# A two-layer decoder trunk: the feed-forward's operands turned by VectorE and DRAM instead of TensorE

## The chip, the cores and the metric

The kernel runs on one core of a Trainium2 chip. The metric is the device time of one execution in microseconds (us), the median of several runs.

## What is computed

The reference is a decoder trunk of depth 2 over 256 tokens with 2048 channels in float32. Layer 0 mixes tokens by stick-breaking attention, layer 1 by a gated DeltaNet; behind each mixer stands a dense SwiGLU feed-forward with 5632 hidden columns. Cut to what matters here:

```python
def swiglu(h, w_gu, w_down):
    gate, up = jnp.split(h @ w_gu, 2, axis=-1)
    return (jax.nn.silu(gate) * up) @ w_down
...
    for i in range(DEPTH):
        kind, j = i % N_MIXERS, i // N_MIXERS
        h = rms_norm(x, mix_norm[i])
...
        x = x + y.astype(x.dtype)
        x = x + swiglu(rms_norm(x, ffn_norm[i]), ffn_w_gu[i], ffn_w_down[i]).astype(x.dtype)
```

## The kernel before

**Products.** Each large product is a list of blocks of 512 output columns for all 256 tokens, and each block a list of units, two 128-row steps of the weights each. A float32 operand is split into a high part in the reduced type fp32r and a low part, the rest; a product is then three: high by high, high by low, low by high. A unit's weights (128 x 1024, 512 KB) come by one DMA on SP's queue (`load`), ScalarE writes their high part, VectorE subtracts to get the low part (`convert`), and TensorE makes 12 matmuls of 512 columns (`product`). The other operand, activations with the channel on the partition, lies in SBUF, split in advance: hTh and hTl for the normed input, and pairs kh and kl for the hidden values.

**The feed-forward.** The 5632 hidden columns are 11 blocks of 512 (j = 0 to 10). For j = 1, 3, 5, 7, 9 gate and up are plain blocks (`ffn_plain`). For the six even j they are made by a seven-product scheme (`ffn_seven`): `sums` forms sums of quarters of the weights on VectorE, and TensorE makes 21 matmuls of 256 columns a unit. Three lanes hold the weights: "a" (tiles w0 to w3) before and after, "s" (the same memory) for the seven-product units, and "b" for the plain units between them, with two raw buffers and two converted ones in the memory of the slabs (tiles slab and slabs). `merge` interleaves s and b units, and OTHERS lists the order of the plain work: a number j is gate and up of block j, a tuple is the part of the down product that uses those blocks.

**Turning the hidden values.** Gate and up leave values with tokens on the partition; the down product needs the hidden column there. At the end of up(j), VectorE has multiplied silu(gate) by up into two tiles of 128 tokens x 512 columns. `transposed_pairs` (L836) then, twice, takes a PSUM bank, has TensorE make four 128x128 transposes against the identity (`tr`, L345), and `split` (L363) reads the bank: ScalarE writes kh, VectorE kl. That is 8 transposes for each j. After the product with up, a seven-product block gives one of its two 128 x 1024 buffers ("duos") back before the transposes, the other behind them.

**What sets the order.** The program is written out in full by a scheduler in Python. Its clock (`self.t`) adds up a cost for each instruction (`spend`); side work runs as tasks that `yield`, and a task goes on when the clock of TensorE has passed what it waits for (`tick`, `Task.pause`). The costs therefore decide where in each engine's queue an instruction stands; they change no instruction. Each engine, and SP, then runs its queue in order and waits on semaphores. Matmuls in fp32r were costed at n / 2400 + 0.006 us for n columns, at least 0.107, and transposes at 0.107.

Of the kernel before, what the change touches and what calls it, by code (L numbers as in the profile page):

```python
# [8 lines left out]
F32 = mybir.dt.float32  # L9
# [22 lines left out]
class Slots:  # L32
# [28 lines left out]
    def put(self, *items):  # L61
        self.free.extend(items)
# [83 lines left out]
class Trunk:  # L146
# [2 lines left out]
    WIDE = 6  # L149
    PAIRS = 6  # L150
    SEVEN = (0, 2, 4, 6, 8, 10)
    OTHERS = (1, 3, (1, 3), 5, (0, 2), (5, 4), 7, (6, 7), 9, (8, 10), (9,))
    LEAD = 10
    SPARE = 4
    BEFORE = 3
# [16 lines left out]
    def __init__(self, ctx, tc, ins, out):  # L172
        self.tc, self.nc, self.ins, self.out = tc, tc.nc, ins, out
        self.tasks = []
        self.cur = None
        self.table = None
        self.t = {"pe": 0.0, "act": 0.0, "dve": 0.0, "sp": 0.0, "dma": self.FIRST}
        self.flags = set()
        self.smalls = {}
        self.persist = ctx.enter_context(tc.tile_pool(name="persist", bufs=1))  # L180
        self.ppool = ctx.enter_context(tc.tile_pool(name="psum", bufs=1, space=PSUM))
        t = self.sb
        self.xs = [t(f"x{n}", [P, NT, NB]) for n in range(4)]
        self.x = [[self.xs[n][:, i, :] for n in range(4)] for i in range(NT)]
        self.hT = []
        for k in range(KT // 2):
            hi, lo = t(f"hTh{k}", [P, 2, S], F32R), t(f"hTl{k}", [P, 2, S], F32R)
            self.hT += [(hi[:, j, :], lo[:, j, :]) for j in range(2)]
        self.pairs = Slots([(t(f"kh{k}", [P, 2, S], F32R), t(f"kl{k}", [P, 2, S], F32R)) for k in range(self.PAIRS)])
        self.slab = self.cut(t("slab", [P, 13 * NB]), NB) + self.cut(self.again("slabs", 8 * NB), NB)  # L190
        self.slabs = Slots(self.slab)
        self.allgm = [[t(f"gm{k}{hl}", [P, NB], F32R) for hl in range(2)] for k in range(1)]
        self.gms = Slots(self.allgm)
        self.lts, self.wide = Slots([]), Slots([])
        self.gdn_memory()
        self.acc = [[self.ppool.tile([P, NB], F32, name=f"acc{b}{i}") for i in range(NT)] for b in range(2)]
        self.banks = Slots([self.ppool.tile([P, NB], F32, name=f"bank{k}") for k in range(4)])
        dram = ctx.enter_context(tc.tile_pool(name="scratch", bufs=1, space=bass.MemoryType.DRAM))
        self.scratch = [dram.tile(s, F32, name=f"scratch{k}") for k, s in enumerate(([32, 1024], [8, P * (P + 1)]))]
        self.n = 0  # L200
        self.weights_memory()

# [134 lines left out]
    def mm(self, out, lhsT, rhs, start=True, stop=True, after=0.0):  # L337
        self.nc.tensor.matmul(out, lhsT, rhs, start=start, stop=stop, skip_group_check=True)  # L338
        n = rhs.free_size()
        if lhsT.dtype == F32R:  # L340
            self.spend("pe", max(0.107, n / 2400 + 0.006), after)
        else:
            self.spend("pe", max(lhsT.free_size(), n) / 600 + 0.005, after)

    def tr(self, out, in_):  # L345
        p = in_.shape[0]
        self.nc.tensor.transpose(out, in_, self.ident[:p, :p])  # L347
        self.spend("pe", 0.107)

    def dma(self, out, in_):  # L350
        self.nc.sync.dma_start(out, in_)
# [468 lines left out]

    def pair_operands(self, ops, src, gain=None, pair=None):

        hi, lo = pair or (yield from self.pairs.get())
        self.split(hi, lo, src, gain)
        left = [2]
        for j, o in enumerate(ops):
            o.hi, o.lo = hi[:, j, :], lo[:, j, :]
            o.ready = True

            def rel():  # L830
                left[0] -= 1
                if left[0] == 0:
                    self.pairs.put((hi, lo))
            o.release = rel

    def transposed_pairs(self, tok, ops, gain=None, put=None):  # L836

        for half in range(2):
# [12 lines left out]
                yield  # L851
            self.banks.put(bank)


    def ffn_units(self, layer, norm, nxt, last, before):

# [6 lines left out]
        def src(c0):  # L863
            return lambda k0, nk: [(gu[:, k0:k0 + nk, c0:c0 + NB], NB)]
# [2 lines left out]
            forms.append(Block(src(j * NB), norm.forms, gate, kind="seven", norm=norm))  # L867
            forms.append(Block(src(HID + j * NB), norm.forms, up, kind="seven", norm=norm))
        for n, what in enumerate(self.OTHERS):
            if isinstance(what, int):  # L870
                gate, up = self.ffn_plain(norm, kops[what])
                others.append(Block(src(what * NB), norm.ops, gate, norm=norm))
                others.append(Block(src(HID + what * NB), norm.ops, up, norm=norm))
                continue
            end = n == len(self.OTHERS) - 1
            rows = [4 * j + k for j in what for k in range(0, 4, 2)]
# [119 lines left out]
    def ffn_plain(self, norm, ops):  # L996
# [9 lines left out]
        def up(acc, free):  # L1006
            for t in range(NT):
                s = hold[t]
                self.stt(s, acc[t], norm.rstd[:, t:t + 1], s, ALU.mult, ALU.mult)
            free()  # L1010
            yield
            yield from self.transposed_pairs(hold, ops, put=lambda: self.slabs.put(*hold))
        return gate, up

    def ffn_seven(self, norm, ops):
# [10 lines left out]
        def up(acc, free):  # L1026
# [3 lines left out]
            for t in range(NT):  # L1030
                g, a = hold[0][:, t * NB:(t + 1) * NB], duo[:, t * NB:(t + 1) * NB]
                self.stt(g, a, norm.rstd[:, t:t + 1], g, ALU.mult, ALU.mult)
                toks.append(g)
            self.duos.put(duo)
            yield
            yield from self.transposed_pairs(toks, ops, put=lambda: self.duos.put(hold[0]))
        return gate, up

    def quarters(self, acc, free):
# [650 lines left out]
```

## Time and profile before

| | |
|---|---|
| median of 3 runs | 2718.93 us (2718.88 to 2719.63) |
| profiled execution | 2723.5 us, span 2721.8 us |
| TensorE busy | 2701.6 us, 99% |
| VectorE busy | 2140.8 us, 79% |
| ScalarE busy | 1488.1 us, 55% |
| DMA queue of SP | 494.10 MB, 60.2% of 16 engines' span |
| granted TensorE clock | 0.999 |

The page names engines PE (TensorE matmul), PEld (its weight loads), DVE (VectorE), ACT (ScalarE), POOL and SP. Matmul records overlap, because matmuls are pipelined: a record's length is not what the matmul costs, and the distance from one start to the next is. Most instructions are recorded at the line of a helper (L338 is every matmul, L347 every transpose, L316 every VectorE subtraction or sum of two tensors, L312 every ScalarE instruction, L503 every weight load), so groups are told apart by the names of their tiles: acc<-slabs,kh is a matmul into an accumulator from a converted b-lane weight and a hidden operand. The first feed-forward lies at about 440 to 1060 us, the DeltaNet stage up to about 2030, and the second feed-forward to the end.

### The profile page before, as it was taken

To read this page: it belongs to the slowest core of one execution; us is meant where nothing else is said; L and a number is where in the kernel's file an instruction comes from. 1 tells how busy PE (TensorE), PEld (TensorE's weight loads), DVE (VectorE), ACT (ScalarE), POOL (GpSimd) and SP (SyncE) were. 2 spreads that over 40 slices of the span, in tenths; PEclk is the share of its full clock that TensorE was granted. 3 is DMA by queue.
4 is the path that set the end of the run, shared out by engine and by line. 5 is a ranking of instruction groups with operands and counts; after the bars stand their busy time and mean duration, and the time that the engine had idled before them with its cause. 6 is when DMAs were issued, how large, how long until landed. Compare 5 with 4: busy or idle time off the path is not lost.

```text
span 2721.8 us, 39670 instructions
## 1 busy us (share of the span) xinstructions
PE 2701.6 (99%) x15018; PEld 2305.6 (85%) x15018; DVE 2140.8 (79%) x3379; ACT 1488.1 (55%) x1969; POOL 11.2 (0%) x95
## 2 busy tenths in 40 slices
PE   9999999999999999999999999999999999999999
PEld 7888888888888888888888888888888888888887
DVE  5555577889889896678878787987678899898975
ACT  5555566455545554555666556655565455455543
POOL 0000000000000000000000000000000000000000
PEclk9999999999999999999999999999999999999999
DMA  6555555656666666656656556556556566666664
GB/s 227 168 162 165 180 184 165 199 185 202 185 194 195 192 201 195 183 167 181 181 149 186 169 149 174 167 162 184 156 181 193 184 194 201 192 187 208 186 204 160
DMA packets 299834, 496.65 MB, mean 182 GB/s; under 512 B 37175, under 2 KB 79482, under 8 KB 299642
## 3 DMA queue, kind: packets, MB, share of 16 engines
q1 hardware_dynamic: 299594, 494.10, 60.2%
q8 instruction: 117, 1.92, 0.3%
q14 instruction: 75, 0.61, 0.1%
q10 hardware_dynamic: 48, 0.02, 0.0%
HBM read 489.33 MB, written 4.72 MB: 182 GB/s over the span
## 4 chain that ended last, share of the span: by engine, by line
PE 88%; DVE 6%; ACT 2%; DMA 2%; issue 2%; ACTq 0%; DVEq 0%
PE acc L338 72%; PE bank L338 13%; DVE w L316 4%; PE bank L347 2%; ACT w L312 1%; DVE slabs L316 1%; DMA slab<-in_ffn_w_down_dram 1%; DVE slab L316 1%; DVE x L316 0%; DMA slab<-in_ffn_w_gu_dram 0%; ACT slabs L312 0%; DVE slab L322 0%; ACT slab L312 0%; DMA x<-in_x_dram 0%; ACT hTh L312 0%
## 5 line engine op out<-in xcount | busy, mean ns | idle before, releaser
L316 DVE TENSOR_TENSOR w<-w,w 128x1024 fp32r<-128x1024 f32 (+2 forms) x750 | 950.0, 1286 | 278.9 <-ACT w L312 276.3
L312 ACT ACTIVATE w<-w 128x1024 fp32r<-128x1024 f32 (+2 forms) x654 | 805.1, 1242 | 379.5 <-PE acc L338 336.5
L338 PE MATMUL acc<-w,hTh 128*128 128x512 f32 (+1 forms) x3296 | 946.3, 371 | 2.8 <-DVE w L316 2.1
L338 PEld LDWEIGHTS acc<-w,hTh 128*128 128x128 f32 x3296 | 594.1, 189 | 108.1 <-DVE w L316 4.8
L338 PE MATMUL acc<-w,hTl 128*128 128x512 f32 (+1 forms) x1648 | 603.5, 366 | 0.0
L312 ACT ACTIVATE slabs<-slab 128x1024 fp32r<-128x1024 f32 x260 | 273.9, 1055 | 400.5 <-PE acc L338 252.4
L316 DVE TENSOR_TENSOR slabs<-slab,slabs 128x1024 fp32r<-128x1024 f32 x260 | 316.7, 1219 | 104.3 <-ACT slabs L312 103.6
L338 PE MATMUL acc<-w,kh 128*128 128x512 f32 x1152 | 361.3, 395 | 0.0
L338 PEld LDWEIGHTS acc<-w,hTl 128*128 128x128 f32 x1648 | 311.4, 189 | 50.9
L338 PE MATMUL acc<-slabs,hTh 128*128 128x512 f32 x1056 | 329.4, 393 | 3.0 <-DVE slab L316 1.7
L338 PE MATMUL acc<-slabs,kh 128*128 128x512 f32 x1024 | 321.7, 393 | 4.8 <-DVE slabs L316 3.3
L316 DVE TENSOR_TENSOR w<-w 128x256 f32<-128x256 f32 (+1 forms) x576 | 289.9, 507 | 6.6 <-DMA w<-in_ffn_w_gu_dram 1.5
L338 PEld LDWEIGHTS acc<-w,kh 128*128 128x128 f32 x1152 | 211.7, 188 | 41.5
L338 PEld LDWEIGHTS acc<-slabs,hTh 128*128 128x128 f32 x1056 | 192.8, 188 | 42.7 <-DVE slab L316 2.1
L338 PEld LDWEIGHTS acc<-slabs,kh 128*128 128x128 f32 x1024 | 187.5, 188 | 46.3 <-DVE slabs L316 8.7
L338 PE MATMUL acc<-w,kl 128*128 128x512 f32 x576 | 224.7, 390 | 0.0
L338 PE MATMUL acc<-slabs,hTl 128*128 128x512 f32 x528 | 205.7, 390 | 0.0
L338 PE MATMUL acc<-slabs,kl 128*128 128x512 f32 x512 | 199.5, 390 | 0.0
L338 PE MATMUL bank<-w,wide 128*128 128x256 f32 x1296 | 180.2, 283 | 0.0
L338 PEld LDWEIGHTS bank<-w,wide 128*128 128x128 f32 x1296 | 166.0, 192 | 0.0
L338 PEld LDWEIGHTS acc<-w,kl 128*128 128x128 f32 x576 | 108.1, 188 | 22.9
L338 PEld LDWEIGHTS acc<-slabs,hTl 128*128 128x128 f32 x528 | 99.1, 188 | 21.2
(203 smaller groups left out, 2373.9 us busy)
## 6 DMA issues: line engine op xcount, KB each, us to landing
w<-in_ffn_w_gu_dram SPq DMA_DIRECT2D x220, 512.0 KB, 4.3
slab<-in_ffn_w_gu_dram SPq DMA_DIRECT2D x132, 512.0 KB, 3.9
w<-in_gdn_w_in_dram SPq DMA_DIRECT2D x129, 512.0 KB, 3.8
slab<-in_ffn_w_down_dram SPq DMA_DIRECT2D x128, 512.0 KB, 4.4
w<-in_sb_w_in_dram SPq DMA_DIRECT2D x96, 512.0 KB, 3.8
w<-in_gdn_w_in_dram SPq DMA_DIRECT2D x128, 256.0 KB, 3.1
w<-in_gdn_w_out_dram SPq DMA_DIRECT2D x64, 512.0 KB, 4.2
w<-in_ffn_w_down_dram SPq DMA_DIRECT2D x48, 512.0 KB, 4.5
```

Source lines behind the costliest of these rows:

```text
L312: self.nc.scalar.activation(out, in_, func, **kw)
L316: self.nc.vector.tensor_tensor(out, a, b, op=op)
L338: self.nc.tensor.matmul(out, lhsT, rhs, start=start, stop=stop, skip_group_check=True)
L347: self.nc.tensor.transpose(out, in_, self.ident[:p, :p])
```

## The change

1. `turned_pairs` takes the place of `transposed_pairs` in both kinds of feed-forward block. VectorE transposes each half of 128 x 512 within blocks of 32 x 32, in place for a plain block and into the up buffer for a seven-product block. DMAs on SP's queue write the result into a DRAM tensor (`ways`, three of them, 1024 x 128) so that the 32 x 32 blocks come to stand where a full transpose has them; other DMAs read it back with the hidden column on the partition. The split then reads SBUF. A plain block takes 8 writes and 4 reads, a seven-product block 4 writes and 2 reads. No PSUM bank is used. Both buffers of a seven-product block are held until the split.
2. OTHERS is spread out: gate or up of another plain block stands between a block's up and the down product that uses it.
3. The scheduler's costs for TensorE: fp32r matmuls n / 2400 + 0.0135 us and at least 0.12, transposes 0.109.

```diff
-    OTHERS = (1, 3, (1, 3), 5, (0, 2), (5, 4), 7, (6, 7), 9, (8, 10), (9,))
+    OTHERS = (1, 3, "gate 5", (1, 3), "up 5", (0, 2), "gate 7", (5, 4), "up 7", "gate 9", (6, 7), "up 9", (8, 10), (9,))
...
+        self.ways = Slots([dram.tile([NT * NB, P], F32, name=f"way{k}") for k in range(3)])
...
-            self.spend("pe", max(0.107, n / 2400 + 0.006), after)
+            self.spend("pe", max(0.12, n / 2400 + 0.0135), after)
...
-        self.spend("pe", 0.107)
+        self.spend("pe", 0.109)
...
+    def turned_pairs(self, tok, stage, ops, put):
+
+
+        way = yield from self.ways.get()
+        halves = lambda pieces: [h for p in pieces for h in self.cut(p, NB)]
+        for s, t in zip(halves(stage), halves(tok)):
+            self.nc.vector.transpose(s, t)
+            self.spend("dve", 0.07 + 0.00104 * NB)
+            self.weave()
+        yield
+
+        n = NT // len(tok)
+        for i, s in enumerate(stage):
+            rows = way[i * n * NB:(i + 1) * n * NB, :].rearrange("(b i) j -> i b j", i=32)
+            for a in range(4):
+                m = slice(32 * a, 32 * a + 32)
+                self.dma(rows[:, :, m], s[m, :].rearrange("p (b j) -> p b j", j=32))
+        yield
+        pairs = []
+        for t in range(NT):
+            for i, l in enumerate(tok):
+                k = 4 // len(tok)
+                at = t * NB + i * k * P
+                self.dma(l.rearrange("p (k s) -> p k s", k=k)[:, :, t * P:(t + 1) * P],
+                         way[at:at + k * P, :].rearrange("(k p) s -> p k s", p=P))
+        for _ in range(2):
+            pairs.append((yield from self.pairs.get()))
+        yield
+        self.ways.put(way)
+        for n, l in enumerate(halves(tok)):
+            self.operands_of(ops[2 * n:2 * n + 2], pairs[n], l.rearrange("p (k s) -> p k s", k=2))
+        put()
...
-            yield from self.transposed_pairs(hold, ops, put=lambda: self.slabs.put(*hold))
+            yield from self.turned_pairs(hold, hold, ops, lambda: self.slabs.put(*hold))
...
-            self.duos.put(duo)
-            yield
-            yield from self.transposed_pairs(toks, ops, put=lambda: self.duos.put(hold[0]))
+            yield
+            yield from self.turned_pairs(hold, [duo], ops, lambda: self.duos.put(hold[0], duo))
```

`operands_of` is the split and the release of `pair_operands`, with the pair given. `ffn_units` reads the strings of OTHERS: "gate 5" appends the gate block of j = 5 alone, "up 5" its up block. The output projections of the mixers keep `transposed_pairs`.

More of the change, by code (lines that the diff above doesn't have):

```diff
@@ L821, in pair_operands, with operands_of @@
     def pair_operands(self, ops, src, gain=None, pair=None):
-        hi, lo = pair or (yield from self.pairs.get())
+        pair = pair or (yield from self.pairs.get())
+        self.operands_of(ops, pair, src, gain)
+    def operands_of(self, ops, pair, src, gain=None):
+        hi, lo = pair
         self.split(hi, lo, src, gain)
@@ L869, in ffn_units @@
         for n, what in enumerate(self.OTHERS):
[L870 to L873, printed above, removed]
+            if not isinstance(what, tuple):
+                j = int(str(what).split()[-1])
+                if "up" not in str(what):
+                    gate, up = self.ffn_plain(norm, kops[j])
+                    others.append(Block(src(j * NB), norm.ops, gate, norm=norm))
+                if "gate" not in str(what):
+                    others.append(Block(src(HID + j * NB), norm.ops, up, norm=norm))
                 continue
```

## The prediction

> **What bounds the kernel now.** I read the page first, then TensorE's timeline, busy time by stretch, the waits of each engine in the first feed-forward (440 to 1060 us), and the chain of waits. The page, engines and chain:
>
> ```profile
> span 2721.8 us, 39670 instructions
> PE 2701.6 (99%) x15018; PEld 2305.6 (85%) x15018; DVE 2140.8 (79%) x3379; ACT 1488.1 (55%) x1969; POOL 11.2 (0%) x95
> PE 88%; DVE 6%; ACT 2%; DMA 2%; issue 2%; ACTq 0%; DVEq 0%
> ```
>
> TensorE has work in all but 20 us of the span and is 88% of the chain: what leaves its queue shortens the program if nothing new makes it wait. But the average hides that VectorE is much fuller in the feed-forward stages (here three stretches of them):
>
> ```profile
> 440.00:660.00 220.00, 217.56 (x1301) 192.66 (x1300) 191.84 (x241) 114.78 (x102) 0.00 (x0) 1.00 0.63 190
> 660.00:860.00 200.00, 198.28 (x1193) 175.90 (x1192) 179.59 (x230) 102.39 (x88) 0.00 (x0) 1.00 0.63 191
> 2250.00:2450.00 200.00, 198.58 (x1203) 176.79 (x1202) 180.36 (x231) 102.16 (x88) 0.00 (x0) 1.00 0.63 193
> ```
>
> Columns: stretch, length, busy PE, PEld, DVE, ACT, POOL, clock, DMA share, GB/s. VectorE is busy 87 to 90% there, and the granted clock is 1.00. The waits in the first feed-forward, TensorE's, ScalarE's, VectorE's and SP's (us in total, times, longest):
>
> ```profile
> PEld acc L338 <- DVE slabs L316: 5.8, 8, 1.3
> PE acc L338 <- DVE slabs L316: 2.4, 5, 0.8
> ACT slabs L312 <- DMA slab<-in_ffn_w_down_dram: 31.2, 13, 6.6
> ACT slabs L312 <- DMA slab<-in_ffn_w_gu_dram: 22.8, 12, 5.8
> ACT kh L312 <- PE bank L347: 24.2, 13, 5.0
> DVE slabs L316 <- ACT slabs L312: 49.7, 36, 5.0
> SPq L503 <- DVE w L316: 414.3, 177, 7.1
> ```
>
> TensorE waits little, and nearly always for one thing: the low parts of weights in the two-buffer lane of plain blocks ("slabs"). One such wait in the chain, in order of time:
>
> ```profile
> 500.51 4.87 DMA slab<-in_ffn_w_gu_dram
> 505.49 1.07 ACT slabs L312
> 506.58 1.24 DVE slabs L316
> 507.86 3.60 PE acc L338 x17
> ```
>
> VectorE frees a raw buffer, the load takes 4.87 us, the split 1.07 and 1.24, and TensorE starts late. So these stages are TensorE-bound with a second chain, load and split, just behind.
>
> **The transposes removed.** Each of the 11 column blocks of a feed-forward was turned by 8 transposes in two groups of four: 22 x 8 = 176, 44 groups. Such transposes by line and form:
>
> ```profile
> L347 PE MATMUL bank<-ident,slab 128*128 128x128 f32 x386 | 63.5, 273 | 0.4 <-ACT slab L312 0.3
> ```
>
> and one group in TensorE's timeline (start, us, instruction):
>
> ```profile
> 538.64 0.62 PE L338 MATMUL acc<-slabs,kh 128*128 128x512 f32 x2
> 539.09 0.40 PE L338 MATMUL acc<-slabs,kl 128*128 128x512 f32 x1
> 539.33 0.60 PE L347 MATMUL bank<-ident,slab 128*128 128x128 f32 x4
> 539.68 0.71 PE L338 MATMUL acc<-slabs,kh 128*128 128x512 f32 x2
> 540.23 0.40 PE L338 MATMUL acc<-slabs,kl 128*128 128x512 f32 x1
> 540.47 0.39 PE L338 MATMUL acc<-w,hTh 128*128 128x256 f32 x2
> ```
>
> A record lasts 273 ns but records overlap; starts decide. Three matmuls take 539.33 - 538.64 = 0.69 us; four transposes and three matmuls take 540.47 - 539.33 = 1.14. So a group costs 0.45 us, and 44 cost **19.8 us**. I take the starts, not the records. The Trainium skill (TensorE: Matmul & The Clock Gate, Part 4: PE-mode transpose) gives a transpose about 275 ns in one kernel's context, and says the clock gate's full rate does not engage for it; the trace agrees on the record (273 ns), and shows a granted clock of 1.00 in these stretches. By that figure as a price, 176 transposes would be 48 us; the starts say 19.8.
>
> One group's place in TensorE's order, before, in the first feed-forward (acc_106 and acc_107 hold a plain block, bank_110 takes the turned values of the block before it):
>
> ```order
> L338 MATMUL acc_104<-w_117,wide_2477 128x256
> L338 MATMUL acc_106<-slabs,hTh_65 128x512 x2
> L338 MATMUL acc_106<-slabs,hTl_66 128x512
> L338 MATMUL acc_107<-slabs,hTh_65 128x512 x2
> L338 MATMUL acc_107<-slabs,hTl_66 128x512
> L347 MATMUL bank_110<-ident,slab 128x128 x4
> ```
>
> and now:
>
> ```order
> L339 MATMUL acc_104<-w_120,wide_2480 128x256
> L339 MATMUL acc_106<-slabs,hTh_65 128x512 x2
> L339 MATMUL acc_106<-slabs,hTl_66 128x512
> L339 MATMUL acc_107<-slabs,hTh_65 128x512 x2
> L339 MATMUL acc_107<-slabs,hTl_66 128x512
> L339 MATMUL acc_106<-slabs,hTh_65 128x512 x2
> ```
>
> The group is gone and the matmuls stand as they did.
>
> **VectorE's transposes added.** Two of 128x512 a block, 44 in all. The kernel has such an instruction already (first row); the split that follows read PSUM and now reads SBUF (kh on ScalarE, kl on VectorE; the nearest SBUF forms are the two "wide" rows):
>
> ```profile
> L1507 DVE STREAM_TRANSPOSE slab<-slab 128x512 f32<-128x512 f32 x10 | 7.0, 696 | 0.8 <-DMA slab<-scratch 0.8
> L316 DVE TENSOR_TENSOR kl<-bank,kh 128x512 fp32r<-128x512 f32 x52 | 35.6, 685 | 15.8 <-ACT kh L312 15.8
> L312 ACT ACTIVATE kh<-bank 128x512 fp32r<-128x512 f32 x52 | 30.9, 593 | 64.5 <-PE bank L347 55.0 <-PE bank L338 9.4
> L316 DVE TENSOR_TENSOR wide<-slab,wide 128x512 fp32r<-128x512 f32 x12 | 8.0, 681 | 0.0
> L312 ACT ACTIVATE wide<-slab 128x512 fp32r<-128x512 f32 x12 | 7.6, 633 | 8.9 <-DVE slab L316 8.9
> ```
>
> 44 x 0.696 = 30.6 us more on VectorE. In the three stretches above it was busy 552 of 620 us, 89%; 22 feed-forward blocks over some 1280 us put 15 us into such a length, which itself shrinks by 10: 93%. The split costs the same on VectorE and 0.04 us more on ScalarE, 1.8 us in all, which its 45% idle time hides. VectorE's place, before:
>
> ```order
> L322 SCALAR_TENSOR_TENSOR slab<-acc_107,rstd_135,slab 128x512
> L316 TENSOR_TENSOR slabs<-slab,slabs 128x1024
> L316 TENSOR_TENSOR w_2930<-w_2930 128x512
> L316 TENSOR_TENSOR kl_82<-bank_110,kh_81 128x512
> L316 TENSOR_TENSOR w_2930<-w_2930 128x256
> ```
>
> and now:
>
> ```order
> L323 SCALAR_TENSOR_TENSOR slab<-acc_107,rstd_138,slab 128x512
> L317 TENSOR_TENSOR slabs<-slab,slabs 128x1024
> L317 TENSOR_TENSOR w_2933<-w_2933 128x512
> L865 STREAM_TRANSPOSE slab<-slab 128x512
> L317 TENSOR_TENSOR w_2933<-w_2933 128x256
> ```
>
> The transposes stand where the first kl stood; kl itself comes some 20 VectorE instructions later. Behind the pair wait the conversions of coming units, for 1.4 us, and behind those TensorE. Bounds: 0 if the idle time takes all, 30.6 if none. Near the lower end, since most of that idle time is back-pressure (VectorE waits for ScalarE, and ScalarE for buffers). TensorE's two rows on slabs, 8.2 us in a feed-forward and 16 in both, would grow by half if they go inversely with VectorE's idle time (11 to 7%): 8 us; I take **+7**.
>
> **The way through DRAM added.** A plain block writes 8 DMAs of 64 KB in 128-byte runs and reads 4; a seven-product block writes 4 and reads 2: 10 x 12 + 12 x 6 = 192 DMAs, 23 MB. Nearest rows, first the issue times on SP of the writes to scratch (min/median/max ns):
>
> ```profile
> L351 SPq DMA_DIRECT2D scratch<-wide x64: 302/430/566, 1212.1 to 1850.4; - x64
> ```
>
> then the DMA issues (count, KB each, us to landing) and the queue's share of 16 engines:
>
> ```profile
> q1 hardware_dynamic: 299594, 494.10, 60.2%
> ...
> slab<-scratch SPq DMA_DIRECT2D x14, 256.0 KB, 4.6
> scratch<-wide SPq DMA_DIRECT2D x64, 16.0 KB, 2.6
> scratch<-slab SPq DMA_DIRECT2D x2, 256.0 KB, 5.8
> ```
>
> SP needs 8 x 0.43 = 3.4 us for a plain block's writes (1.7 for a seven's), 1.7 (0.9) for its reads. A write lands after 2.6 to 5.8 us, I take 3.5; a read after about 4.6. Turn, writes, reads, split: 1.4 + 3.4 + 3.5 + 1.7 + 4.6 + 1.3 = 16 us, where transposes and split took about 2 (0.45 + 0.45 + 0.593 + 0.685). SP's place, before (loads of gate and up columns for block 3):
>
> ```order
> L503 DMA w_116<-in_ffn_w_gu_dram 128x2x512
> L503 DMA slab<-in_ffn_w_gu_dram 128x2x512
> L503 DMA w_2930<-in_ffn_w_gu_dram 128x2x512
> L503 DMA slab<-in_ffn_w_gu_dram 128x2x512
> L503 DMA w_116<-in_ffn_w_gu_dram 128x2x512 x2
> ```
>
> and now:
>
> ```order
> L504 DMA w_119<-in_ffn_w_gu_dram 128x2x512
> L352 DMA way_116<-slab 32x16x32 x8
> L504 DMA slab<-in_ffn_w_gu_dram 128x2x512
> L504 DMA w_2933<-in_ffn_w_gu_dram 128x2x512
> L504 DMA slab<-in_ffn_w_gu_dram 128x2x512
> L504 DMA w_119<-in_ffn_w_gu_dram 128x2x512
> L352 DMA slab<-way_116 128x2x128 x4
> ```
>
> Four loads stand between writes and reads. A feed-forward has 264 loads of 512 KB (22 column blocks of 8, 88 for the down product) in some 640 us, 2.4 us a load; four are 10 us, so the reads should find the writes landed and not hold SP. Operands have time too: by the new OTHERS a block's gate or up (8 units of 12 matmuls at 0.69 / 3 us = 22 us, and the seven-product units between) stands ahead of the product that uses them. What suffers is the load behind 8 writes: 3.4 us of issue where 2.4 are between loads makes it 1.0 us late. By bytes the way adds 23 / 494 x 60 = 3 points to the DMA engines' 63%. The slab conversions by line:
>
> ```profile
> L312 ACT ACTIVATE slabs<-slab 128x1024 fp32r<-128x1024 f32 x260 | 273.9, 1055 | 400.5 <-PE acc L338 252.4
> ```
>
> 25 of some 130 in a feed-forward wait for their load, a fifth. 44 bursts (writes and reads), 1.3 slab loads behind each, 1.0 us, a fifth: 11 us more at ScalarE, of which TensorE feels a part, as now (54 us of such waits at ScalarE, 8 of TensorE's). I take **+4 us**; bounds -3 (ScalarE's 24.2 us of waiting for transposes go, and what is queued behind kh on ScalarE comes earlier) to +33 (the third rival).
>
> The Trainium skill (DMA: Bandwidth & Descriptors, Specifications) speaks against it: under 512 B a transfer becomes read-modify-write. Counting the written half double, an estimate by that page, the way would add 4 points of DMA share, not 3, and in that proportion +5 us, not +4; no row here separates the price of a 128-byte run.
>
> **The measured TensorE times.** They only move instructions. Attention's order on TensorE stays; in the DeltaNet stage small products come some matmuls earlier against ScalarE and VectorE. There TensorE's largest wait is
>
> ```profile
> PEld bank L338 <- issue: 19.5, 66, 0.4
> ```
>
> changes of shape, which stay. Slack exists and shrinks: -4 to +8, I take 0.
>
> Sum: -19.8 + 7 + 4 + 0 = -8.8. The profiled execution took 2723.5 us and would take 2714.7; it lies 4.6 above the median of the runs, 2718.93, which would become **2710 us**, and alone, with half or one and a half of the two costs, 2705 to 2715. About 0.2% (5.4 us) is what a measurement can tell from no change.
>
> **The rivals.**
> Full cover: no new wait: 2718.9 - 19.8 = 2699. For it: TensorE waits so little now, and ScalarE loses a wait of up to 5.0 us. Against: 7% is all that VectorE would have left.
>
> VectorE gives it back: the bursts meet low parts that are already late; two thirds of 30.6 paid, 20 us: 2719, no change. For it: TensorE's waits end on VectorE. Against: 11% idle now.
>
> Slower: the bursts delay slab loads, the chain shown at 500.51. If each of 22 write bursts costs TensorE 1.5 us, 33 us: 2718.9 - 19.8 + 33 = 2732. It decides from 19.8 / 22 = 0.9 us a block. For it: a fifth of these loads have no slack. Against: SP's 414 us of waiting for buffers.
>
> Transposes cost their records: 176 x 0.273 = 48 us: 2671. Against: the starts, 0.45 us for four.
>
> **How the numbers follow.** Forecast 0.42, full cover 0.18, given back 0.22, slower 0.16, records 0.02. Faster 0.42 + 0.18 + 0.02 = 0.62, within 0.2% 0.22, slower 0.16. The range 2698 to 2724 takes in the first three and leaves out the records' case and most of the slower one.
>
> **What would show it.** L347 loses 176 transposes, TensorE's busy time about 20 us; VectorE's transposes near 0.7 us and its share in feed-forward about 93%; TensorE's waits on slabs up by half; SP waiting little for the way's writes. Wrong it is if ScalarE's waits for slab loads double, if kh waits for the way's reads, or if DeltaNet grows by over 8 us.

## The result, and the profile after

The changed kernel takes 2746.13 us (median of 4 runs, 2744.51 to 2752.63) against 2718.9: ratio 1.0102, 95% interval [1.0088, 1.0115]. It is slower by 27 us, where 2710 was forecast. The profiled execution took 2745.91 us. Its page, engines, chain and DMA queue:

```profile
span 2744.2 us, 39637 instructions
PE 2697.5 (98%) x14842; PEld 2290.9 (83%) x14842; DVE 2164.6 (79%) x3423; ACT 1491.4 (54%) x1971; POOL 11.2 (0%) x95
q1 hardware_dynamic: 415306, 517.18, 61.7%
PE 70%; DVE 17%; DMA 6%; issue 3%; ACT 3%; SPq 1%; ACTq 0%; DVEq 0%; POOL 0%; POOLq 0%
```

TensorE has 176 instructions fewer, as the change says, and yet its share of the chain fell from 88% to 70%: it now waits for others, for VectorE (6 to 17%) and for DMAs (2 to 6%). The same three stretches of the feed-forwards as before:

```profile
440.00:660.00 220.00, 214.21 (x1264) 189.43 (x1263) 193.41 (x245) 113.33 (x99) 0.00 (x0) 0.99 0.66 204
660.00:860.00 200.00, 196.13 (x1160) 172.51 (x1159) 179.16 (x229) 102.17 (x90) 0.00 (x0) 1.00 0.68 208
2250.00:2450.00 200.00, 195.74 (x1146) 171.90 (x1146) 177.92 (x228) 102.48 (x89) 0.00 (x0) 1.00 0.68 207
```

TensorE gets through fewer matmuls in each (1264 for 1301, 1160 for 1193, 1146 for 1203), the DMA engines are busier (0.63 to 0.66 and 0.68), and VectorE is not fuller than before: 550.5 of 620 us, 89%. The waits in the first feed-forward, 440 to 1060 us:

```profile
ACT slabs L313 <- DMA slab<-in_ffn_w_gu_dram: 51.1, 21, 6.4
ACT slabs L313 <- DMA slab<-in_ffn_w_down_dram: 35.1, 18, 6.7
PEld acc L339 <- DVE slabs L317: 11.8, 13, 1.7
ACT kh L313 <- DMA slab<-way: 7.7, 5, 3.7
PE acc L339 <- DVE slabs L317: 6.9, 10, 1.2
PE acc L339 <- ACT slabs L313: 2.7, 2, 2.5
SPq L352 <- DMA way<-slab: 0.3, 1, 0.3
```

ScalarE waits 86.2 us for slab loads, 54.0 before; TensorE's two rows on the slabs' low parts go from 8.2 to 18.7. SP hardly waits for the way's writes when it reads (0.3 us), as was reckoned. The largest of TensorE's waits in this stage ends at about 568 us. ScalarE's conversions of slabs before it, VectorE's subtractions and TensorE's two waits (start, us, instruction; in brackets the idle time before it, and for whom):

```profile
552.88 1.06 ACT L313 ACTIVATE slabs<-slab 128x1024 fp32r<-128x1024 f32 x1 [1.00 <-DMA slab<-in_ffn_w_gu_dram]
560.38 1.06 ACT L313 ACTIVATE slabs<-slab 128x1024 fp32r<-128x1024 f32 x1 [6.43 <-DMA slab<-in_ffn_w_gu_dram]
566.94 1.06 ACT L313 ACTIVATE slabs<-slab 128x1024 fp32r<-128x1024 f32 x1 [5.50 <-DMA slab<-in_ffn_w_gu_dram]
...
553.15 1.18 DVE L317 TENSOR_TENSOR slabs<-slab,slabs 128x1024 fp32r<-128x1024 f32 x1
556.80 1.21 DVE L317 TENSOR_TENSOR slabs<-slab,slabs 128x1024 fp32r<-128x1024 f32 x1
...
568.05 0.50 PE L339 MATMUL acc<-slabs,hTh 128*128 128x512 f32 x1 [2.47 <-ACT slabs L313]
569.31 0.57 PE L339 MATMUL acc<-slabs,hTh 128*128 128x512 f32 x1 [0.76 <-DVE slabs L317]
```

and SP's queue in this time (start, us of the row, first instruction and count):

```profile
549.24 0.37 SPq L504 DMA_DIRECT2D slab<-in_ffn_w_gu_dram  x1
549.66 4.68 SPq L352 DMA_DIRECT2D way<-slab  x8
554.43 0.46 SPq L504 DMA_DIRECT2D w<-in_ffn_w_gu_dram  x1
554.99 0.41 SPq L504 DMA_DIRECT2D slab<-in_ffn_w_gu_dram  x1
556.30 0.37 SPq L504 DMA_DIRECT2D w<-in_ffn_w_gu_dram  x1
556.72 5.46 SPq L352 DMA_DIRECT2D way<-slab  x4
562.27 0.57 SPq L504 DMA_DIRECT2D slab<-in_ffn_w_gu_dram  x1
```

This is the chain of load and split that stood just behind TensorE before, now with the way's bursts in it. The two raw slabs are filled and freed in turn. VectorE frees one at 554.33 us (553.15 + 1.18) and the other at 558.01. The loads that fill them start at 554.99, behind the eight writes, and at 562.27, behind the four: 0.66 and 4.26 us after the slab came free. ScalarE waits for both, and TensorE behind ScalarE.

Eight writes of 64 KB hold SP 4.68 us here and four of 128 KB 5.46, where 3.4 and 1.7 had been reckoned; the medians of all bursts in this trace are 5.4 (10 of eight) and 5.2 (12 of four). The writes' issues (min/median/max ns):

```profile
L352 SPq DMA_DIRECT2D way<-slab x128: 327/554/3596, 470.8 to 2684.3; - x128
```

The median is 0.55 us, but an issue can take 3.6. It is SP's queue that is late.

To see where the time lies, I took for each of TensorE's matmuls the distance from its start to the next start in the trace, less the usual distance for its columns (227 ns for 512, 120 for 256, 109 for a transpose), and summed this by stage. TensorE's lost time, us, with the median time of each run:

| kernel | attention | 1st feed-forward | DeltaNet | 2nd feed-forward | time |
|---|---|---|---|---|---|
| before | 15.7 | 11.7 | 27.5 | 10.7 | 2718.9 |
| after | 14.8 | 25.4 | 41.3 | 25.5 | 2746.1 |

28.5 us more in the feed-forwards and 13.8 in DeltaNet, less 0.9 and the 19.8 of the transposes: 21.6, and the spans differ by 22.4.

### The profile page after: what moved, and what is told of

The parts are those of the page before. It is cut to its first block, busy times and chain, and to the rows that moved or that the text cites. A ratio compares the mean times of both kernels' runs of the same rounds, so it can differ in the third digit from the quotient of the medians.

```text
span 2744.2 us, 39637 instructions
## 1 busy us (share of the span) xinstructions
PE 2697.5 (98%) x14842; PEld 2290.9 (83%) x14842; DVE 2164.6 (79%) x3423; ACT 1491.4 (54%) x1971; POOL 11.2 (0%) x95
## 4 chain that ended last, share of the span: by engine, by line
PE 70%; DVE 17%; DMA 6%; issue 3%; ACT 3%; SPq 1%; ACTq 0%; DVEq 0%; POOL 0%; POOLq 0%
PE acc L339 58%; PE bank L339 10%; DVE w L317 8%; DVE slabs L317 3%; DMA slab<-in_ffn_w_gu_dram 2%; PE bank L348 2%; DVE slab L317 1%; ACT w L313 1%; DMA slab<-way 1%; DMA slab<-in_ffn_w_down_dram 1%; SPq L352 1%; ACT slabs L313 1%; DVE slab L323 1%; DMA lt<-scratch 1%; DVE slab L865 0%
## 5 line engine op out<-in xcount | busy, mean ns | idle before, releaser
L339 PE MATMUL acc<-slabs,hTh 128*128 128x512 f32 x1056 | 335.2, 396 | 15.7 <-DVE slabs L317 8.6
L339 PEld LDWEIGHTS acc<-slabs,hTh 128*128 128x128 f32 x1056 | 195.9, 190 | 61.3 <-DVE slabs L317 15.2
L339 PEld LDWEIGHTS acc<-w,kl 128*128 128x128 f32 x576 | 108.4, 188 | 25.7 <-DVE kl L323 2.1
```

## The experiments

All of them were timed beside the kernel before, which took 2720.8 to 2722.0 us there (e17 has a single time). The intervals are about 0.1% of the time to each side, so a difference of less than some 3 us between two kernels says nothing by itself. The letters of the theories hold within one group: e1 to e4, e5 to e8, e9 to e17. "The way" is the 192 DMAs to DRAM and back, "the planner" the scheduler in Python.

### The parts of the change: e1 to e4

e1, the kernel before with the new TensorE times only:

```diff
-            self.spend("pe", max(0.107, n / 2400 + 0.006), after)
+            self.spend("pe", max(0.12, n / 2400 + 0.0135), after)
...
-        self.spend("pe", 0.107)
+        self.spend("pe", 0.109)
```

> Only the scheduler's TensorE prices are the new ones; operands are turned by TensorE, in the old order of the plain work. Theory A (the prices move DeltaNet's instructions early against ScalarE, VectorE and DMA, and TensorE waits, with short drops of its clock behind): the 14 us that the DeltaNet stretch lost appear here, 2719 + 14 = 2733 us, with the feed-forward as before. Rival B (DeltaNet lost time through something that the feed-forward left behind, and the prices only reorder): 2719 us within 4.

Measured: 2729.3 us, ratio 1.0032 [1.0022, 1.0042]: 8.5 us slower without any new work. TensorE's lost time in DeltaNet goes from 27.5 to 33.8 us.

e2, the changed kernel with the old TensorE times (the same lines the other way round):

> The changed kernel with the old TensorE prices. Theory A: DeltaNet's 14 us are gone and the feed-forwards keep their 28 us of new waits against 20 saved: 2746 - 14 = 2732 us. Rival B: the prices do nothing, 2746 us within 4. A third case, that the true prices help the feed-forward: over 2740 us with a faster DeltaNet.

Measured: 2744.6 us, 1.0085 [1.0071, 1.0099]. DeltaNet has most of its time back (lost 30.2), but the feed-forwards lose 28.1 and 29.9. Within the change the new times are worth 1.5 us by these medians and 4.6 by the ratios (1.0102 and 1.0085), neither clear of noise: DeltaNet loses 11.1 us by them, and the feed-forwards lose 7.1 less. What follows is therefore built on e2.

e3, the kernel before with OTHERS spread out:

> Only the spread-out order of the plain work; TensorE turns, old prices. Theory A: the order as such costs nothing, 2719 us within 4. Rival C (the new order brings more plain units in a row, whose two raw buffers are reloaded too late, and that is what TensorE waits for in the feed-forward): some 10 us or more of new waits on slabs, 2729 us or more.

Measured: 2721.5 us, 1.0002 [0.9993, 1.0010]. The new list costs nothing.

e4, e2 with the turning left out whole:

```diff
-        way = yield from self.ways.get()
...
-            self.nc.vector.transpose(s, t)
...
-                self.dma(rows[:, :, m], s[m, :].rearrange("p (b j) -> p b j", j=32))
...
-                self.dma(l.rearrange("p (k s) -> p k s", k=k)[:, :, t * P:(t + 1) * P],
-                         way[at:at + k * P, :].rearrange("(k p) s -> p k s", p=P))
```

> The changed kernel with old prices, and the turning left out altogether: the split reads the unturned values, so the down product gets other operands. No transposes on TensorE or VectorE, no way through DRAM. Theory A: the prediction's 19.8 us come in full, 2719 - 20 = 2699 us. Rival C: the order's waits stay, 2710 us or more.

Measured: 2709.8 us, 0.9956 [0.9942, 0.9969]. Even with nothing in their place, the 176 transposes are worth 11.3 us and not 19.8: the feed-forwards lose 15.4 and 13.8 us where they lost 11.7 and 10.7. ScalarE's waits for slab loads in the first one are 91.7 us (54.7 and 37.0), more than the changed kernel's 86.2, with none of the way's DMAs in SP's queue: their sum doesn't tell a load that starts late from a TensorE that got ahead. The turning itself costs 2744.6 - 2709.8 = 34.8 us, and the rest of the study is about these. (e4 also has an order of its own: beside e2, some 890 of TensorE's instructions, 420 of VectorE's and 270 of ScalarE's stand elsewhere. No run separates that from the work.)

### VectorE or the way: e5 to e8

e5 leaves out the DMAs of e2, e6 its transposes:

```diff
# e5
-                self.dma(rows[:, :, m], s[m, :].rearrange("p (b j) -> p b j", j=32))
...
-        for n, l in enumerate(halves(tok)):
+        for n, l in enumerate(halves(stage)):
# e6
-            self.nc.vector.transpose(s, t)
-            self.spend("dve", 0.07 + 0.00104 * NB)
-            self.weave()
+            pass
...
-        for i, s in enumerate(stage):
+        for i, s in enumerate(tok):
```

> The changed kernel with the old TensorE prices, with VectorE's 44 transposes of 128x1024 kept and the way through DRAM left out (both directions): the split reads the stage, whose values are turned only inside 32x32 squares, so the down product gets operands that are not fully transposed. Beside it stand e2_turn_old_prices (2744.6 us: transposes and way) and e4_not_turned (2709.8 us: neither); the 35 us between them are to be shared out. Theory A (SP's queue: issuing the way's 192 DMAs holds up the feed-forward's weight loads): the 30.6 us of VectorE are mostly hidden, 2715 us. Theory B (VectorE: the queue of conversions and splits gets later by each block's four transposes of 0.7 us): 2735 us or more. Theory C (the way's traffic on the DMA engines, and reads that come late to ScalarE's kh conversions): 2715 us, as A.

> The changed kernel with the old TensorE prices, with the way's 128 writes and 64 reads kept and VectorE's transposes left out: what goes out is the unturned piece, so the down product gets operands whose 32x32 squares are not turned. Theory A: 2738 us, nearly all of the 35 us. Theory B: 2715 us. Theory C: 2738 us, as A; A and C are told apart by the next kernel. If the two halves together come to clearly less than 35 us (both under 2722 us), they add up only where they meet: transposes that delay the conversions, and loads that come late for the same conversions.

Measured: e5 2714.6 us, 0.9976 [0.9967, 0.9986]; e6 2712.9 us, 0.9968 [0.9958, 0.9978]. (The transposes are 44 of 128 x 512, two a block, and not the sizes and counts that e5's expectation names.) Against e4 the transposes alone cost 4.8 us and the way alone 3.1. All three theories fall as they stand: neither half costs much alone, and together they cost 34.8. SP's issues are as long in e6 as in the changed kernel:

```profile
L352 SPq DMA_DIRECT2D way<-slab x128: 418/544/3881, 465.7 to 2655.5; - x128
```

e7 has GpSimd issue the way, e8 puts a step of the scheduler behind each of its DMAs:

```diff
# e7, writes and reads
-                self.dma(rows[:, :, m], s[m, :].rearrange("p (b j) -> p b j", j=32))
+                self.wdma(rows[:, :, m], s[m, :].rearrange("p (b j) -> p b j", j=32))
...
+        self.nc.gpsimd.dma_start(out, in_)
# e8, writes and reads
                 self.dma(rows[:, :, m], s[m, :].rearrange("p (b j) -> p b j", j=32))
-        yield
+                yield
```

> The changed kernel with the old TensorE prices, complete, and the way's 192 DMAs issued by GpSimd (11 us busy in the whole span) in place of SP; SP has only the other loads and stores. Traffic, bytes and runs are the same. Theory A: the loads no longer stand behind the way's issues, 2720 us (within 10 us of e4_not_turned's 2709.8). Theory B: 2744 us, nothing changes, since VectorE has the same work. Theory C: 2740 us or more, since the same packets share the 16 DMA engines, and a GpSimd issue that takes longer makes the turned operands later still.

> The changed kernel with the old TensorE prices, complete, and a step of the scheduler (a yield) after each of the way's DMAs in place of one after all writes of a block and one after all reads, so that weight loads can be issued between them. Theory A, if it is the burst (SP busy for 4 to 8 writes in a row) that makes loads late: 2728 us. Theory B and theory C: 2743 us, within 4 us of e2_turn_old_prices, since work and traffic are the same; a longer way could even make it slower.

Measured: e7 2733.5 us, 1.0046 [1.0034, 1.0058]; e8 2870.0 us, 1.0548 [1.0535, 1.0562]. In e7 the first feed-forward loses 16.9 us and not 28.1, so the way's place in SP's queue seems to matter, as A has it, though e7's order is another too. It does not reach 2720, because TensorE waits at the end of each feed-forward, 4.3 and 5.0 us at a time, for operands that come late. In e8 the way stretches so far that the down product has to wait for its operands, as ScalarE's and TensorE's waits in its first feed-forward show:

```profile
ACT kh L313 <- DMA slab<-way: 36.2, 6, 13.7
...
PE acc L339 <- ACT kh L313: 34.2, 3, 16.9
```

Spacing was no remedy; the length of the way counts as well.

### The order held fast: e9 to e12

e5 and e6 had changed more than the work. The planner adds up costs, so an edit that drops a cost also moves instructions: between e2 and e6 TensorE's whole order and SP's weight loads are the same, but 60 of VectorE's instructions and 38 of ScalarE's stand elsewhere, and in e6 most of the way stands 2 to 4 loads earlier in SP's queue. e9, e10 and e11 keep e2's costs, and with them its order to the instruction:

```diff
# e9
-            self.nc.vector.transpose(s, t)
+            self.nc.vector.transpose(s[:32, :32], t[:32, :32])
# e10: the planner is charged the whole DMA, an eighth or less is issued
+                self.way_dma(o, v, lambda: self.nc.sync.dma_start(o[:, ::8, :], v[:, ::8, :]))
...
+                self.way_dma(o, v, lambda: self.nc.sync.dma_start(o[:32, :1, :], v[:32, :1, :]))
# e11: the planner is charged as in e2, GpSimd issues the whole
+                self.way_dma(o, v, lambda: self.nc.gpsimd.dma_start(o, v))
```

> e2_turn_old_prices (2744.6 us) with its order of all four queues kept to the instruction, and each of the 44 transposes cut to one 32x32 square (what leaves for DRAM is left nearly unturned); the way is complete. e5 and e6 showed that the transposes alone cost 4.9 us and the way alone 3.1, where both together cost 35. Theory E (they meet: the way's issues on SP make loads late, and only a VectorE that is 93% busy cannot make that up): with VectorE's 28 us gone, 2716 us. Theory D (order: leaving out the transposes or the way changed the planner's sums, and 40 to 60 of ScalarE's and VectorE's instructions stood elsewhere in e5 and e6; it is their place in e2 that costs): order is the same, so it stays over 2735 us.

> e2_turn_old_prices with its order of all four queues kept, and each of the way's 192 DMAs cut to an eighth or less of its runs (4 of 32 or 2 of 16 blocks of 32 columns out, 32 rows back; the values that come back are only partly turned ones). VectorE's transposes are complete. Theory E: SP issues in 0.4 us each and is not held back, loads land earlier, 2718 us. Theory D: over 2735 us. If it is between, 2725 to 2735, both have a share.

> e2_turn_old_prices complete and with its order of VectorE, ScalarE, TensorE and of SP's other DMAs kept; only the way's 192 DMAs stand in GpSimd's queue in place of SP's. Bytes and runs are the same. Theory E with SP's issue as its part of the way: feed-forward stalls fall from 28 and 30 us to 17 each, and the last block's operands come some us later (GpSimd takes 0.66 to 0.71 us an issue), 2726 us. Theory E with the traffic as its part: 2740 us or more. Theory D: as e2 or slower, 2745.

Measured: e9 2731.5 us, 1.0035 [1.0022, 1.0048]; e10 2718.1, 0.9991 [0.9982, 1.0000]; e11 2725.2, 1.0013 [1.0004, 1.0022]. In e2's order the transposes cost 13.1 us, the way's bytes and issues 26.5, and 19.4 go when GpSimd issues the way, with all bytes still moved and a longer median issue:

```profile
L883 POOL DMA_DIRECT2D way<-slab x128: 652/656/817, 467.0 to 2661.0; - x128
```

So the way's time in SP's queue looks like the largest part. (The edit changes more than the issuer: the page of e11 has the way in a DMA queue of its own, in 8704 packets, where it adds some 115,700 packets to SP's in the changed kernel.) But e9 also misses its 2716 by 15 us, and it differs from e6 (2712.9) by order and by 44 small squares: the order itself had to be tried.

e12 is e7 with block 9, the last plain one, transposed by TensorE as before:

```diff
+            if last:
+                yield from self.transposed_pairs(hold, ops, put=lambda: self.slabs.put(*hold))
+                return
             yield from self.turned_pairs(hold, hold, ops, lambda: self.slabs.put(*hold))
```

> e7_way_on_gpsimd (2733.5 us) with the last plain block of each feed-forward (block 9, whose operands ScalarE awaited 12 us at the end of the first feed-forward) transposed by TensorE as before the change: 32 transposes in 8 groups more on TensorE, +3.6 us; the two waits at the ends (5.3 and 6.9 us of TensorE's time, and the clock at half for 3.4 and 6.8 us after them) go: 2719 us, about the kernel before. If the waits at the ends only move to the block ahead of the last: 2730 us or more. Theory D makes no statement on it.

Measured: 2716.6 us, 0.9982 [0.9973, 0.9991]. The waits at the two ends are gone but for 1.1 us. It is 0.2% faster than the kernel before and 1.1% faster than the changed one: a version that beats both, barely.

### The order by itself: e13 to e17

e13 is e2 with all its work, but the planner isn't told of the transposes:

```diff
             self.nc.vector.transpose(s, t)
-            self.spend("dve", 0.07 + 0.00104 * NB)
-            self.weave()
```

> e2_turn_old_prices complete (44 whole transposes, whole way on SP), but the planner is not told of the transposes' 0.6 us each, so that all four queues stand in the order of e6_way_only to the instruction. Theory D (place in the queues is worth the 18.7 us between e9's 2731.5 and e6's 2712.9): 2712.9 + 13.1 for VectorE's work, 2726 us. Theory E (no order is better than the other; VectorE's work and the late loads meet): as e2, 2744 us or more.

Measured: 2719.1 us, 0.9995 [0.9985, 1.0004]. The same instructions in e6's order are 25.5 us faster than in e2's. All medians by order and work, us:

| work | order of e2 | order of e6 |
|---|---|---|
| transposes whole, way by SP | 2744.6 (e2) | 2719.1 (e13) |
| transposes small or none, way by SP | 2731.5 (e9) | 2712.9 (e6) |
| transposes whole, way by GpSimd | 2725.2 (e11) | 2717.6 (e16) |
| transposes whole, way an eighth | 2718.1 (e10) | |

Knowing of 0.6 us more of VectorE's time for each transpose, the planner lets the tasks that turn a block go on a little later. One of these bursts, the last of a seven-product block in the first feed-forward, in SP's queue of e2, with the subtractions that free the raw slabs and ScalarE's conversions behind it:

```profile
966.76 0.37 SPq L504 DMA_DIRECT2D slab<-in_ffn_w_down_dram  x1
967.18 5.82 SPq L352 DMA_DIRECT2D way<-slab  x4
973.09 0.57 SPq L504 DMA_DIRECT2D slab<-in_ffn_w_down_dram  x1
```

```profile
965.52 1.21 DVE L317 TENSOR_TENSOR slabs<-slab,slabs 128x1024 fp32r<-128x1024 f32 x1
966.99 1.21 DVE L317 TENSOR_TENSOR slabs<-slab,slabs 128x1024 fp32r<-128x1024 f32 x1
...
972.77 1.06 ACT L313 ACTIVATE slabs<-slab 128x1024 fp32r<-128x1024 f32 x1 [2.36 <-DMA slab<-in_ffn_w_down_dram]
978.01 1.06 ACT L313 ACTIVATE slabs<-slab 128x1024 fp32r<-128x1024 f32 x1 [4.19 <-DMA slab<-in_ffn_w_down_dram]
```

and the same burst in e13:

```profile
955.37 0.37 SPq L504 DMA_DIRECT2D slab<-in_ffn_w_down_dram  x1
956.24 0.37 SPq L504 DMA_DIRECT2D w<-in_ffn_w_gu_dram  x1
958.59 3.08 SPq L352 DMA_DIRECT2D way<-slab  x4
961.77 0.57 SPq L504 DMA_DIRECT2D w<-in_ffn_w_gu_dram  x1
962.43 1.64 SPq L504 DMA_DIRECT2D slab<-in_ffn_w_down_dram  x2
```

```profile
960.99 1.22 DVE L317 TENSOR_TENSOR slabs<-slab,slabs 128x1024 fp32r<-128x1024 f32 x1
962.46 1.22 DVE L317 TENSOR_TENSOR slabs<-slab,slabs 128x1024 fp32r<-128x1024 f32 x1
...
968.92 1.06 ACT L313 ACTIVATE slabs<-slab 128x1024 fp32r<-128x1024 f32 x1 [3.04 <-PE acc L339]
970.21 1.06 ACT L313 ACTIVATE slabs<-slab 128x1024 fp32r<-128x1024 f32 x1 [0.23 <-DMA slab<-in_ffn_w_down_dram]
```

In e2 VectorE frees the raw slabs at 966.73 and 968.20 us. The first load goes out ahead of the burst (ScalarE's 2.4 us for it aren't SP's doing); the second stands behind it and starts at 973.09, 4.9 us late. ScalarE waits 4.2 us for it, and TensorE loses 0.8 and 1.0 us at 979 and 980. In e13 the burst takes 3.1 us and not 5.8, and is over at 961.7, before the slabs come free at 962.2 and 963.7; their loads start within 0.3 us, ScalarE waits 0.2 us, and TensorE loses nothing there.

The last four put these edits together:

```diff
# e14 is e11, e15 and e17 are e7, with
+            if last:
+                yield from self.transposed_pairs(hold, ops, put=lambda: self.slabs.put(*hold))
+                return
# e15 and e17 are e7, e16 is e11, with
-            self.spend("dve", 0.07 + 0.00104 * NB)
-            self.weave()
```

> e11_gpsimd_same_order (2725.2 us) with the last plain block of each feed-forward transposed by TensorE, as e12_gpsimd_last_by_tensor (2716.6 us) but with the planner's sums of e11. If e12's gain over e7 (17 us) comes here too: 2712 us. If only the waits at the two ends go (0.6 and 1.0 us in e11's trace) while 3.6 us of TensorE's transposes come: 2726 us.

> e12_gpsimd_last_by_tensor (2716.6 us) with VectorE's transposes not told to the planner, as in e13. Theory D, if the better place is that of e6 on this queue too: 2706 to 2712 us. Theory E: 2716 us, as e12; a plan that knows less could also be worse, 2722.

> e13_transposes_not_planned (2719.1 us) with its order of VectorE, ScalarE, TensorE and of SP's other DMAs kept to the instruction, and the way's 192 DMAs in GpSimd's queue. In e2's order the same edit was worth 19 us (e11). If place and SP's bursts are one cause (a burst costs where it stands ahead of a load that is due), there is little left to gain: 2714 to 2722 us, the way's own latency included. If SP's issue costs 19 us wherever it stands: 2700 us. If GpSimd's slower issue brings the operands too late for conversions that stand earlier here: 2730 us or more.

> The program of e15_unplanned_gpsimd_last_by_tensor once more, for its profile. Theory: its conversions of turned operands stand 2 to 7 instructions earlier in ScalarE's queue than e2's, while GpSimd issues the way slower than the planner reckons; then ScalarE waits over 40 us for the way's reads in each feed-forward (2.5 in e2), everything behind it is late, and TensorE stalls by several us at a time, with the clock at half after it: about 2760 us. If ScalarE's waits for the way are under 15 us, the cause is another and stays open.

Measured: e14 2725.7 us, 1.0014 [1.0005, 1.0023]; e15 2764.5, 1.0161 [1.0145, 1.0177]; e16 2717.6, 0.9989 [0.9980, 0.9998]; e17 2762.7. In the better place, taking the way off SP's queue is worth 1.5 us, within the noise, and not 19.4. That is a net figure: ScalarE's waits for the way's reads, over the whole run, grow with it from 22.4 us (e13) to 38.6 (e16), and fall from 10.5 (e2) to 3.2 (e11).

To see it for all bursts and not for one, I took for each of the 256 slab loads of the two feed-forwards behind the first two the time from the end of the subtraction that frees its raw slab to the load's start on SP:

| kernel | started over 2 us late | late in total, us | time |
|---|---|---|---|
| before | 1 | 14.3 | 2718.9 |
| after | 16 | 76.0 | 2746.1 |
| e2 old times | 17 | 77.4 | 2744.6 |
| e9 small transposes | 17 | 74.4 | 2731.5 |
| e10 small way | 6 | 36.4 | 2718.1 |
| e6 way only | 7 | 52.4 | 2712.9 |
| e13 not planned | 6 | 42.4 | 2719.1 |
| e4, e11, e16 | 1 | 14.1 to 14.3 | 2709.8, 2725.2, 2717.6 |

So place and bursts are largely one cause: in e6's order fewer loads are due behind a burst, and with GpSimd no more are late than in the kernel before. The better place alone is worth 25.5 us, GpSimd alone 19.4, and both together 27.0, so 17.9 us are common to the two. Two things don't follow from late loads: e9 has as many as e2, and is 13.1 us faster with VectorE relieved; and between e11 and e16, where loads start as early as before, the order is still worth 7.6 us. What that part is, was not tried.

e15 is the other side of the order, as its program once more (e17) shows for the first feed-forward:

```profile
ACT kh L313 <- DMA slab<-way: 41.6, 10, 7.6
```

There ScalarE waits for the way's reads, 41.6 us here and 44.0 in the second feed-forward, against 2.5 in e2's first. That fits conversions of turned operands that stand too early in ScalarE's queue for a way that GpSimd brings later than the planner reckons. e14 has e12's edit without e12's gain, since e11 hardly waited at the ends (0.6 and 1.0 us). So e12's 0.2% is a plan that happens to fit, not a property of the edit.

TensorE's lost time of the runs that carry the argument, us:

| kernel | attention | 1st feed-forward | DeltaNet | 2nd feed-forward | time |
|---|---|---|---|---|---|
| e1 new times only | 14.1 | 11.4 | 33.8 | 10.9 | 2729.3 |
| e2 old times | 15.6 | 28.1 | 30.2 | 29.9 | 2744.6 |
| e4 nothing turned | 15.6 | 15.4 | 27.2 | 13.8 | 2709.8 |
| e6 way only | 15.7 | 19.9 | 27.3 | 15.8 | 2712.9 |
| e9 small transposes | 14.8 | 21.8 | 30.2 | 25.7 | 2731.5 |
| e10 small way | 15.2 | 18.3 | 25.9 | 17.9 | 2718.1 |
| e11 GpSimd | 15.6 | 20.5 | 27.8 | 23.9 | 2725.2 |
| e13 not planned | 14.7 | 21.6 | 26.3 | 18.7 | 2719.1 |
| e16 both | 15.5 | 18.1 | 28.3 | 18.4 | 2717.6 |

## Why the prediction was wrong

By these runs, beside 2721.1 us for the kernel before, the change is made up so: 11.3 us less without the transposes (e4, in its own order), 9.3 more for the turning in a good order (e4 to e13), 25.5 more for the order that it in fact gets (e13 to e2), 1.5 more for the new times (e2 to after). That is 25.0 us; beside its own 2718.9 the change costs 27.2, since the groups were timed apart. The 1.5 lies within the noise. By the steps of the prediction:

- **The bound** was read rightly: TensorE, with load and split just behind. Its consequence was not drawn for the first term.
- **-19.8 for the transposes.** The price by starts holds (their records would have given 48), and 176 instructions went. But e4 gives 11.3, and the feed-forwards' lost time grows by 6.8 us with no new work at all: the term was 8.5 us too large. That a chain just behind takes part of what is removed fits this, and ScalarE's longer waits for loads that start no later than before; e4's own order may have a share.
- **+7 for VectorE.** One transpose took 0.689 us, 0.696 was reckoned. Measured 6.2 us in e6's order (e6 to e13) and 13.1 in e2's (e9 to e2). The size was right for one order. The share of 93% did not come: it was reckoned on stages that get shorter, and they got longer.
- **+4 for the way is the step that failed**, in its sentence "What suffers is the load behind 8 writes: 3.4 us of issue where 2.4 are between loads makes it 1.0 us late". The issue was priced from a row of 16 KB writes (0.43 us), which gives 54 us for all writes; in the changed kernel the bursts took 114. The four writes of 128 KB, reckoned at 1.7 us, took 5.2 at the median, nearly as long as eight of 64 KB. And the lateness was spread evenly: 44 bursts, 1.3 loads each, 1.0 us late make 57 us, of which a fifth was counted. Loads in fact became 62 us later in total (14.3 to 76.0), so that sum was met by chance, but 16 of them are over 2 us late, where 1.0 each had been reckoned. (By the forecast's own ratio, 8 us at TensorE for 54 at ScalarE, its 11 us would have been 1.7 and not 4.) In the order that the kernel has, the way costs 26.5 us (e10), within the bounds of -3 to +33 that were given, and most of it goes when SP doesn't issue it (19.4, e11). In e6's order it costs 3.1 (e6 less e4, whose orders differ), near the forecast; but SP's issues are as long there, so that agreement is luck.
- **What moves.** The prediction saw that kl comes some 20 VectorE instructions later and that the bursts stand among the loads, and priced neither as a change of order. The place was worth 25.5 us, as much as the whole way in the bad order. The planner reckons 0.46 us for each issue on SP, whatever its size (`issue + 0.46` in `transfer`), so four writes of 128 KB are 1.8 us to it and it saw no harm.
- **+0 for the measured times** was too kind: +8.5 alone (e1), just past the bound of +8, and 1.5 to 4.6 within the change. More exact times for one engine did not make a better plan.
- **The marks set beforehand.** "If ScalarE's waits for slab loads double": they grew by 60% in the first feed-forward (54.0 to 86.2), and doubled in e2 (119.9). It was a poor mark, since e4 has 91.7 without the way. "If kh waits for the way's reads": it does, 29.4 us in the whole run. "If DeltaNet grows by over 8 us": its lost time grew by 13.8. Here e1 and e2 show the new times at work (6.3 us on the kernel before, 11.1 between e2 and after). The granted clock was about 0.5 for 10 us of that stage (from 1481 and from 1870 us), before for 3, so some 3 of the 13.8 us are the clock's. Which of its instructions came too early was not tried.
- **The rivals.** The slower one had the mechanism, slab loads held up by bursts and a point of 0.9 us a block; 26.5 us over 22 blocks is 1.2, and with the transposes 34.8 is 1.6. It was given a chance of 0.16 on the strength of "SP's 414 us of waiting for buffers". That idle time is real, but it lies between loads that are each due at a moment, and does not help the load behind a burst.

What stays open: how the 7.1 us between e10 and e11 divide between the way's full traffic and GpSimd's longer way, what the 7.6 us of order between e11 and e16 are, and what limit holds single issues on SP for up to 3.6 us. The Trainium skill (DMA: Bandwidth & Descriptors, Specifications) says that transfers under 512 B become read-modify-write, which would make the way's traffic dearer; no run here separates that from the number of runs.

## What to carry to other kernels

When a change sends DMAs through a queue that also loads weights, price the whole burst from rows of the same size and run length, and ask which load stands behind it and when that is due; the queue's idle share says nothing about that. Where a planner sets the order, a new cost in its sums is a change of its own: run the new work in the old order and the old work in the new order before blaming the work. And what is taken from an engine that only just bounds a stage is worth less than its time; the run that removes it and puts nothing in its place tells how much.

## What was not expected of the hardware

**SP's issue time is not set by the bytes.** Writes of 64 and 128 KB in 128-byte runs took 0.55 us at the median and up to 3.6, and a weight load of 512 KB, in runs of 2 KB, 0.37 us in the rows above. With an eighth of the runs and of the bytes (e10):

```profile
L883 SPq DMA_DIRECT2D way<-slab x128: 302/427/2009, 471.2 to 2652.5; - x128
```

GpSimd issued the same full-size writes in 0.65 to 0.82 us, with no such tail (e11). Of the 21 writes of the changed kernel that held SP for over 1 us, 17 ended within 0.2 us before an earlier DMA landed; at moments up to 3 us earlier or later, 4 on average would. So the long issues seem to wait for earlier DMAs to finish; no run tried it.

**The clock falls after a short wait.** Three stretches of the changed kernel, at TensorE's wait shown above, and one of e9 (columns as before, the clock is the third number from the end):

```profile
560.00:568.00 8.00, 5.58 (x25) 4.22 (x23) 2.16 (x3) 2.12 (x3) 0.00 (x0) 1.00 1.13 273
569.50:573.00 3.50, 3.50 (x9) 2.78 (x9) 3.43 (x6) 3.00 (x5) 0.00 (x0) 0.52 0.60 168
573.00:580.00 7.00, 7.00 (x52) 6.59 (x51) 6.80 (x8) 5.61 (x7) 0.00 (x0) 1.00 0.84 254
```

```profile
1074.20:1077.60 3.40, 3.40 (x10) 2.62 (x9) 1.22 (x1) 0.00 (x0) 0.00 (x0) 0.50 0.64 98
```

In the changed kernel TensorE sat idle 2.47 and 0.76 us with one matmul between, and from 569.5 us on the granted clock was 0.52 for 3.5 us. In e9 a single wait of 2.08 us ended at 1072.76, and the clock was 0.50 for the 3.4 us from 1074.2. The Trainium skill (TensorE: Matmul & The Clock Gate, Why this matters for your kernels) advises against TensorE gaps of more than about 3 us; these traces show the fall after 3.2 us of idling in two pieces and after a single wait of 2.1. So such a wait costs more than its own length.
